# A two-layer decoder trunk: the indexer's queries of the first 128 tokens are no longer formed

## The chip, the cores and the metric

The kernel runs on one core of one Trainium2 chip. The metric is device time in microseconds (us) of one execution; a median of several executions is given. All times of single instructions come from one profiled execution.

## The reference, cut to what matters

The reference is two layers of a decoder for 512 tokens of width 1024, in float32. Each layer is a feed-forward block, a mixer with three attention branches that read one common input projection, and a second feed-forward block. The branch that matters here is A, a sparse attention: an indexer scores every key for every query, and each query attends only to its 128 best-scored keys.

```python
topk = min(INDEX_TOPK, S // 4)        # S = 512, so 128
...
qi = rope(qi.reshape(B, S, IDX_HEADS, IDX_DIM), cos, sin)     # 8 heads of 64
ki = rope(ki, cos, sin)
...
causal = s_pos[None, :] <= t[:, None]
logits = jnp.einsum('bqhd,bsd->bqhs', qib, ki)
iscore = jnp.einsum('bqhs,bqh->bqs', jax.nn.relu(logits).astype(jnp.float32), wib.astype(jnp.float32))
iscore = jnp.where(causal[None], iscore, -jnp.inf)
_, idx = lax.top_k(iscore, topk)
...
valid = (idx <= t[None, :, None])[:, None]
```

Query t has t + 1 causal keys. For the first 128 queries that is at most 128, so all of their causal keys are among the 128 picked ones, whatever the scores.

## The kernel before

**Tiles.** The 512 tokens are four tiles of 128 (`NT = 4`, tile number `t`). The width of 1024 is eight chunks of 128 (`KD = 8`, chunk number `k`). Activations and weights are kept as a high part and a low part (`hi`, `lo`, in the format F32R), and each float32 product is three matmuls: low times high, high times high, high times low.

**The mixer.** It first projects the normalised input, group of columns by group: `qi` (the indexer's queries, 512 columns), `ki` (the indexer's key, the values of branch B and the indexer's weights, 328 columns), `b`, `vc`, `c0` and so on. `project` loads the weights of a group in four pieces (`load_w`: one DMA on SyncE into `raw`, then ScalarE makes `hi` at L220 and VectorE makes `lo` at L221). There are four buffers each for `raw`, `hi` and `lo`, so the pieces of the next group can be split only once the last tile of the group before has read the old ones. Then, for each tile `t`, `project` issues 8 chunks of three matmuls (L755 to L757), 24 in all, into one of two PSUM banks.

**After a tile of `qi`.** ScalarE copies the bank out with the norm's factor (L919), GpSimd rotates it (`rope`, four instructions, L767 to L772), ScalarE and VectorE split it (L819, L820) and, some steps later, TensorE turns it with 8 transposes of 128x128 (L826, two PSUM banks of the tag `tr`). Eight casts then write the turned heads into the tiles of `qis`; `nc.any` at L829 divides them between ScalarE and VectorE. The counter `ready["i"]` goes up by one at each turned tile, of `qi` and of `ki`.

**The norm.** `n.advance` runs one stage after the first tile of `qi` (mean square, L309) and one after the second (broadcast, L327).

**Who reads `qis`.** Only `index_scores`, which starts when `ready["i"]` has its full count. Its loop already begins with tile 1: the mask of tile 0 is the causal mask, `masks = [causal_mask(0)]`.

**Order.** The order on each engine is the order in which the code issues instructions. A loop advances the projections by two chunks at a time and puts attention work and delayed steps (`defer`, counted in such steps) between them.

Of the kernel before, what the change touches and what calls it, by code (L numbers as in the profile page):

```python
# [23 lines left out]
NT = T // P  # L24
# [55 lines left out]
def trunk_kernel(ctx, tc, xt_in, pos_in, ng_in, wgu, wdn, wgrp, wgate, wbr_s, wbr_c, wo, qkg_in, lam_in, subg_in, out):  # L80
# [18 lines left out]
    def bank(tag="mm"):  # L99
        return ps.tile([P, 512], F32, tag=tag, name=nm(tag), bufs=BANKS[tag])  # L100

    def slot(dt=F32, tag="h", cols=512):
        return big.tile([P, cols], dt, tag=tag, name=nm(tag), bufs=SLOTS)

    def temp(tag, dt=F32, cols=512, bufs=2):
        return (phase[-1] if tag in ("p0", "p1", "pt", "e", "u") else tmp).tile([P, cols], dt, tag=tag, name=nm(tag), bufs=bufs)
# [105 lines left out]
    def load_w(src, cols, pieces=1):  # L212

        raw = wp.tile([P, WCOLS], F32, tag="raw", name=nm("raw"), bufs=RAW)
        hi = wp.tile([P, WCOLS], F32R, tag="hi", name=nm("hi"), bufs=HL)
        lo = wp.tile([P, WCOLS], F32R, tag="lo", name=nm("lo"), bufs=HL)
        for i in range(pieces):
            sl = slice(i * cols // pieces, (i + 1) * cols // pieces)
            nc.sync.dma_start(raw[:, sl], src[:, sl])
            S.activation(hi[:, sl], raw[:, sl], AF.Copy)  # L220
            V.tensor_tensor(lo[:, sl], raw[:, sl], hi[:, sl].bitcast(F32), op=ALU.subtract)  # L221
        return hi, lo
# [506 lines left out]
    def mixer(l, n, nxt, aside):  # L729
# [9 lines left out]
            tiles = [slot() for _ in range(NT // n_)]  # L739
            return lambda t: tiles[t // n_][:, (t % n_) * cols:(t % n_ + 1) * cols]  # L740

        def project(name):

            w_cols = len(GROUPS[name])
            kk_ = 2
            ws = []
            for k in range(0, KD, kk_):
                ws.append(load_w(wgrp[l, :, goff[name] + k * w_cols:goff[name] + (k + kk_) * w_cols], kk_ * w_cols))
            for t in range(NT):
                o = bank()  # L750
                for k in range(KD):
                    wh, wl = ws[k // kk_]
                    sl = slice((k % kk_) * w_cols, (k % kk_ + 1) * w_cols)
                    xh, xl = n.h[k][:, t * P:(t + 1) * P], n.l[k][:, t * P:(t + 1) * P]
                    PE.matmul(o[:, :w_cols], xl, wh[:, sl], start=k == 0, stop=False)  # L755
                    PE.matmul(o[:, :w_cols], xh, wh[:, sl], start=False, stop=False)  # L756
                    last_dense[0] = PE.matmul(o[:, :w_cols], xh, wl[:, sl], start=False, stop=k == KD - 1)  # L757
                    if k % 2 and k < KD - 1:
                        yield t, None
                yield t, o  # L760

        def rope(v, t, nh):

            a = sm.tile([P, 8, 16], F32, name=nm("ra"), tag="ra", bufs=2)
            b = sm.tile([P, 8, 16], F32, name=nm("rb_"), tag="rb_", bufs=2)
            ct = rc[:, t:t + 1, :].to_broadcast([P, nh, 16])
            G.tensor_tensor(a[:, :nh], v[:, :, :16], ct, op=ALU.mult)  # L767
            s0 = rs[:, t:t + 1, :8].to_broadcast([P, nh, 8])
            s1 = rs[:, t:t + 1, 8:].to_broadcast([P, nh, 8])
            G.tensor_tensor(b[:, :nh, :8], v[:, :, 8:16], s0, op=ALU.mult)  # L770
            G.tensor_tensor(b[:, :nh, 8:], v[:, :, :8], s1, op=ALU.mult)
            G.tensor_tensor(v[:, :, :16], a[:, :nh], b[:, :nh], op=ALU.add)  # L772
# [41 lines left out]
        def to_heads(v, nh, t, dst, lag, done):  # L814

            s = phase[-1].tile([P, 8, 2, HD], F32R, tag="st", name=nm("st"), bufs=ST)

            def split():
                S.activation(s[:, :nh, 0, :], v[:, :nh], AF.Copy)  # L819
                V.tensor_tensor(s[:, :nh, 1, :], v[:, :nh], s[:, :nh, 0, :].bitcast(F32), op=ALU.subtract)  # L820
                defer(LAG_H, turn)

            def turn():
                ps_ = [bank("tr") for _ in range(0, nh, 4)]
                for h in range(nh):
                    PE.transpose(ps_[h // 4][:, h % 4 * P:(h % 4 + 1) * P].bitcast(F32R),  # L826
                                 s[:, h].rearrange("p a d -> p (a d)"), ident_r)
                for h in sorted(range(nh), key=lambda h: (h % 4, h)):
                    nc.any.tensor_copy(dst[h][:, t * P:(t + 1) * P], ps_[h // 4][:, h % 4 * P:(h % 4 + 1) * P])  # L829
                done[0] += 1  # L830

            defer(lag, split)

        def swapped(src):
            d = slot(F32R)
            nc.sync.dma_start(d[:HD, :].bitcast(F32), src[HD:, :].bitcast(F32))
            nc.sync.dma_start(d[HD:, :].bitcast(F32), src[:HD, :].bitcast(F32))
            return d

        def scores(q, k1, k2, i):  # L840

            o = bank("sc")[:, :(i + 1) * P]
            ql = q[:, i * P:(i + 1) * P]
            PE.matmul(o, ql, k2[:, :(i + 1) * P], start=True, stop=False)  # L844
            PE.matmul(o, ql, k1[:, :(i + 1) * P], start=False, stop=True)
            return o
# [63 lines left out]
        va = phase[-1].tile([P, NT, HD], F32, tag="va", name=nm("va"), bufs=1)  # L910

        def dense_qi():
            for t, o in project("qi"):
                if o is None:
                    yield True
                    continue
                n.advance(last_dense[0])
                v = temp("t1", bufs=T1).rearrange("p (h d) -> p h d", d=HD)
                S.activation(v, o.rearrange("p (h d) -> p h d", d=HD), AF.Copy, scale=n.rn[:, t, :])  # L919
                rope(v, t, 8)  # L920
                to_heads(v, 8, t, qis, LAG_I, ready["i"])
                yield True

        def dense_ki():
            for t, o in project("ki"):
                if o is None:
                    yield True
                    continue
                v = temp("t1", bufs=T1).rearrange("p (h d) -> p h d", d=HD)
                S.activation(v[:, 0], o[:, :HD], AF.Copy, scale=n.rn[:, t, :])  # L930
                rope(v[:, :1], t, 1)
                to_heads(v, 1, t, kis, LAG_I, ready["i"])
                S.activation(vb(t), o[:, 64:320], AF.Copy, scale=n.rn[:, t, :])
                V.tensor_scalar(wi[:, t, :], o[:, 320:328], n.rn[:, t, :], 512 ** -0.5, op0=ALU.mult, op1=ALU.mult)
                yield True

        ready = {k: [0] for k in ("i", "b", "c0", "c1", "a")}

        def dense_qk(name, rows, qs, ks):
            for t, o in project(name):  # L940
                if o is None:
                    yield True
                    continue
                v = normed(o, t, [(base + rows[0], 4), (base + rows[1], 4)])
                to_heads(v, 8, t, qs + ks, LAG_N, ready[name])
                yield True
# [28 lines left out]
        def index_scores():  # L975
            ki2 = swapped(kis[0])
            for i in range(1, NT):
                w = (i + 1) * P
                acc = slot()
                for h in range(8):  # L980
                    o = scores(qis[h], kis[0], ki2, i)
                    r = temp("t2")
                    S.activation(r[:, :w], o, AF.Relu)
                    V.scalar_tensor_tensor(acc[:, :w], r[:, :w], wi[:, i, h:h + 1],
                                           causal[:, 512 - w:] if h == 0 else acc[:, :w], op0=ALU.mult, op1=ALU.add)
                    yield 1
                iscore.append(acc)
# [149 lines left out]
        def finished(b):  # L1137
# [10 lines left out]
        picks = choose()  # L1148
        ka2 = []
        work = deque([  # L1150
            (lambda: ready["i"][0] == 2 * NT, index_scores()),
            (lambda: ready["b"][0] == NT,
             attend("b", qb, kb, None, causal_mask, lambda j, h: vb(j)[:, h * HD:(h + 1) * HD], on_b)),
            (lambda: ready["c0"][0] == NT, attend_c(qc0, kc0, 0, on_c[:2])),
# [44 lines left out]
        for d in range(KD):  # L1199
# [3 lines left out]
            o = bank()  # L1203
# [16 lines left out]
    for l in range(DEPTH):  # L1220
        n1, n2 = Norm(3 * l + 1), Norm(3 * l + 2)
        n3 = Norm(3 * l + 3) if l + 1 < DEPTH else None
        aside = dram.tile([P, KD, T], F32, name=nm("aside"))
        with stage(f"ff{l}0"):
            ffn(l, 0, n, n1, aside, xt_in if l == 0 else None)
        with stage(f"mix{l}"):
            mixer(l, n1, n2, aside)
        with stage(f"ff{l}1"):
            ffn(l, 1, n2, n3)
        n = n3  # L1230
# [50 lines left out]
```

## Time and profile before

| | us |
|---|---|
| median of 3 executions | 2314.67 |
| lowest and highest of them | 2313.87 and 2317.65 |
| the profiled execution | 2315.78 |
| its span, first to last instruction | 2314.0 |
| TensorE (PE) busy in it | 2286.2 |
| VectorE (DVE) busy | 1721.5 |
| ScalarE (ACT) busy | 1117.9 |
| GpSimd (POOL) busy | 386.3 |

The span is what the trace shows; the execution's own time is a little longer. Busy time of TensorE is time in which at least one matmul is under way. The records of matmuls overlap: the next one starts before the record of the one before has ended, so the distance between starts, not the length of a record, is what a matmul takes of TensorE's time.

### The profile page before, as it was taken

The page shows a single profiled execution, that of the slowest core. Times are in us where ns is not written, and L with a number is a line of the kernel's source. Part 1 is how long each engine was busy: PE and PEld are TensorE (multiplying, and loading weights), DVE is VectorE, ACT ScalarE, POOL GpSimd, SP SyncE. Part 2 cuts the span into 40 slices and gives each one's busy share as a digit, 9 for nine tenths or more (in the row PEclk, how much of TensorE's full clock was granted, in tenths as well). Part 3 has the DMA queues.
Part 4 walks back from the last instruction along what each step waited for, and adds up shares of the span by engine and source line. Part 5 has one row for each costly group of instructions (what it writes and reads, how often), then busy time and mean ns, then how long its engine had stood idle before and what let it go on. Part 6 is the DMA issues. An engine that isn't in the chain of part 4 may idle for free.

```text
span 2314.0 us, 36117 instructions
## 1 busy us (share of the span) xinstructions
PE 2286.2 (99%) x13669; PEld 2013.8 (87%) x13669; DVE 1721.5 (74%) x3126; ACT 1117.9 (48%) x2129; POOL 386.3 (17%) x509
## 2 busy tenths in 40 slices
PE   9999999999999999999999999999999999999999
PEld 7899988887878889999889999888888887899997
DVE  7777765788875778777687777647889666777774
ACT  5444435666433444444444444446764344544442
POOL 0111101455010111101011101024641110110100
PEclk9999999999999999999999999999999999999999
DMA  4665524323232456555256555232322224655551
GB/s 161 176 162 157 143 68 137 101 76 101 74 96 73 141 146 164 159 147 153 66 156 167 157 146 156 84 125 74 101 74 82 88 91 137 159 153 147 157 137 64
DMA packets 111646, 286.74 MB, mean 124 GB/s; under 512 B 13168, under 2 KB 13168, under 8 KB 111472
## 3 DMA queue, kind: packets, MB, share of 16 engines
q1 hardware_dynamic: 90016, 246.00, 33.6%
q0 software_dynamic: 20736, 37.76, 9.7%
q8 instruction: 107, 1.75, 0.3%
q10 hardware_dynamic: 720, 0.68, 0.1%
q14 instruction: 67, 0.55, 0.1%
HBM read 270.76 MB, written 6.29 MB: 120 GB/s over the span
## 4 chain that ended last, share of the span: by engine, by line
PE 85%; DVE 7%; DMA 3%; ACT 2%; issue 1%; POOL 1%; SPq 0%; ACTq 0%; DVEq 0%; POOLq 0%
PE mm L227 11%; PE mm L229 10%; PE mm L228 10%; PE sc L227 8%; PE sc L229 8%; PE sc L228 8%; PE tr L227 5%; PE tr L229 5%; PE tr L228 5%; PE mm L755 4%; PE mm L756 3%; PE mm L757 3%; DMA h<-h 1%; PE sc L844 1%; DVE lo L344 1%
## 5 line engine op out<-in xcount | busy, mean ns | idle before, releaser
L227 PE MATMUL mm<-h,hi 128*128 128x512 f32 x1216 | 481.9, 396 | 1.4 <-DVE h L547 0.8
L229 PE MATMUL mm<-h,lo 128*128 128x512 f32 x1216 | 475.4, 391 | 4.3 <-DVE lo L344 4.3
L228 PE MATMUL mm<-h,hi 128*128 128x512 f32 x1216 | 474.5, 390 | 0.0
L452 POOL DMA_DIRECT2D sa<-in_wgu x144 | 126.8, 1051 | 931.4 <-DMA sa<-in_wgu 428.8
L229 PEld LDWEIGHTS mm<-h,lo 128*128 128x128 f32 x1216 | 228.3, 188 | 54.9 <-DVE lo L344 6.1
L344 DVE TENSOR_TENSOR lo<-raw,hi 128x1024 fp32r<-128x1024 f32 (+1 forms) x198 | 232.9, 1179 | 57.7 <-ACT hi L341 57.0
L227 PEld LDWEIGHTS mm<-h,hi 128*128 128x128 f32 x1216 | 228.4, 188 | 48.8 <-issue 4.8
L227 PE MATMUL sc<-h,hi 128*128 128x256 f32 (+1 forms) x832 | 265.4, 319 | 0.0
L229 PE MATMUL sc<-h,lo 128*128 128x256 f32 (+1 forms) x832 | 264.3, 318 | 0.0
L228 PEld LDWEIGHTS mm<-h,hi 128*128 128x128 f32 x1216 | 228.6, 188 | 41.0
L228 PE MATMUL sc<-h,hi 128*128 128x256 f32 (+1 forms) x832 | 264.1, 317 | 0.0
L341 ACT ACTIVATE hi<-raw 128x1024 fp32r<-128x1024 f32 (+1 forms) x198 | 200.7, 1020 | 92.0 <-PE tr L228 58.1
L227 PE MATMUL tr<-h,hi 128*128 128x256 f32 (+1 forms) x704 | 214.1, 304 | 5.0 <-DVE h L283 5.0
L229 PE MATMUL tr<-h,lo 128*128 128x256 f32 (+1 forms) x704 | 213.7, 303 | 0.0
L228 PE MATMUL tr<-h,hi 128*128 128x256 f32 (+1 forms) x704 | 213.5, 303 | 0.0
L220 ACT ACTIVATE hi<-raw 128x1024 fp32r<-128x1024 f32 (+2 forms) x136 | 139.6, 1029 | 99.2 <-PE mm L228 66.7
L221 DVE TENSOR_TENSOR lo<-raw,hi 128x1024 fp32r<-128x1024 f32 (+2 forms) x136 | 173.3, 1276 | 17.1 <-ACT hi L220 16.2
L755 PE MATMUL mm<-hi,h 128*128 128x512 f32 (+2 forms) x448 | 172.4, 385 | 0.0
L227 PEld LDWEIGHTS sc<-h,hi 128*128 128x128 f32 x832 | 159.3, 191 | 12.8 <-issue 0.3
L228 PEld LDWEIGHTS sc<-h,hi 128*128 128x128 f32 x832 | 159.2, 191 | 12.1
L229 PEld LDWEIGHTS sc<-h,lo 128*128 128x128 f32 x832 | 159.2, 191 | 11.1 <-DVE lo L570 0.4
L757 PE MATMUL mm<-lo,h 128*128 128x512 f32 (+2 forms) x448 | 167.0, 373 | 0.0
(337 smaller groups left out, 5063.8 us busy)
## 6 DMA issues: line engine op xcount, KB each, us to landing
raw<-in_wgu SPq DMA_DIRECT2D x102, 512.0 KB, 4.8
sa<-in_wgu SPq DMA_DIRECT2D x72, 512.0 KB, 3.9
sa<-in_wgu POOLq DMA_DIRECT2D x144, 256.0 KB, 5.8
raw<-in_wdn SPq DMA_DIRECT2D x128, 256.0 KB, 4.7
raw<-in_wgate SPq DMA_DIRECT2D x48, 512.0 KB, 3.5
raw<-in_wgrp SPq DMA_DIRECT2D x40, 512.0 KB, 4.5
a<-in_wgu SPq DMA_DIRECT2D x72, 256.0 KB, 5.1
raw<-in_wdn SPq DMA_DIRECT2D x32, 384.0 KB, 3.5
```

The source lines that it names most:

```text
L220: S.activation(hi[:, sl], raw[:, sl], AF.Copy)
L221: V.tensor_tensor(lo[:, sl], raw[:, sl], hi[:, sl].bitcast(F32), op=ALU.subtract)
L227: PE.matmul(o, ah, bl, start=first, stop=False, skip_group_check=onto)
L228: PE.matmul(o, ah, bh, start=False, stop=False, skip_group_check=onto)
L229: last_mm[0] = PE.matmul(o, al, bh, start=False, stop=last, skip_group_check=onto)
L341: S.activation(self.h, self.src, AF.Copy)
L344: V.tensor_tensor(self.l, self.src, self.h.bitcast(F32), op=ALU.subtract)
L452: G.dma_start(self.sa[:, j * 512:(j + 1) * 512], src[:, 1536:], accum_op=ALU.add)
L755: PE.matmul(o[:, :w_cols], xl, wh[:, sl], start=k == 0, stop=False)
L756: PE.matmul(o[:, :w_cols], xh, wh[:, sl], start=False, stop=False)
L757: last_dense[0] = PE.matmul(o[:, :w_cols], xh, wl[:, sl], start=False, stop=k == KD - 1)
L844: PE.matmul(o, ql, k2[:, :(i + 1) * P], start=True, stop=False)
```

## The change

The projection of `qi` runs over tiles 1 to 3 only, so for the tokens 0 to 127 the 24 matmuls, the copy out, the rotation, the split, the 8 transposes and the 8 casts are not issued, in each of the two layers. The weights of `qi` are loaded and split as before. The indexer's scores wait for seven turned tiles in place of eight. The output is the same function as before.

```diff
-        def project(name):
+        def project(name, tiles=range(NT)):
...
-            for t in range(NT):
+            for t in tiles:
                 o = bank()
...
         def dense_qi():
-            for t, o in project("qi"):
+            for t, o in project("qi", range(1, NT)):
...
-            (lambda: ready["i"][0] == 2 * NT, index_scores()),
+            (lambda: ready["i"][0] == 2 * NT - 1, index_scores()),
```

The order of the instructions shows what this makes of each engine. On TensorE, in the first layer, this is the end of the third projected tile of `qi` and what follows it, of before (`mm` is the PSUM bank of a projected tile, `hi` and `lo` the weights, `h` the activations, 128x512 the shape of the result):

```order
L757 MATMUL mm_3955<-lo_3860,h_3762 128x512
L755 MATMUL mm_4009<-hi_3841,h_3557 128x512
L756 MATMUL mm_4009<-hi_3841,h_3556 128x512
L757 MATMUL mm_4009<-lo_3842,h_3556 128x512
...
L826 MATMUL tr_4022<-ident_r,st_3954 128x128 x4
L826 MATMUL tr_4023<-ident_r,st_3954 128x128 x4
...
L757 MATMUL mm_4009<-lo_3860,h_3762 128x512
L755 MATMUL mm_4087<-hi_4064,h_3557 128x328
```

And the same place with the change:

```order
L757 MATMUL mm_3955<-lo_3860,h_3762 128x512
L755 MATMUL mm_4033<-hi_4010,h_3557 128x328
L756 MATMUL mm_4033<-hi_4010,h_3556 128x328
L757 MATMUL mm_4033<-lo_4011,h_3556 128x328
L755 MATMUL mm_4033<-hi_4010,h_3573 128x328
```

One block of 24 matmuls with 8 transposes in its middle is gone; the first matmul of `ki` (128x328) stands right behind the third projected tile, and apart from the numbers of the buffers every other row of TensorE stands as before, in both layers.

On ScalarE, from the copy of the second projected tile (L919) to the split of the second half of the `ki` weights, before (`tr` is a bank with turned heads, `raw` a loaded piece of weights, `st` the split tile ahead of its transposes):

```order
L919 ACTIVATE t_735_3946<-mm_3914,rn_3896 128x512
L329 ACTIVATE rb_3944<-tr_3941 128x512
...
L819 ACTIVATE st_3954<-t_735_3946 128x8x64
L919 ACTIVATE t_742_4000<-mm_3955,rn_3896 128x512
L220 ACTIVATE hi_4064<-raw_4063 128x656
L220 ACTIVATE hi_4070<-raw_4069 128x656
...
L819 ACTIVATE st_4008<-t_742_4000 128x8x64
L220 ACTIVATE hi_4076<-raw_4075 128x656
L220 ACTIVATE hi_4082<-raw_4081 128x656
L919 ACTIVATE t_749_4054<-mm_4009,rn_3896 128x512
```

With the change:

```order
L919 ACTIVATE t_735_3946<-mm_3914,rn_3896 128x512
L329 ACTIVATE rb_3944<-tr_3941 128x512
L220 ACTIVATE hi_4010<-raw_4009 128x656
L220 ACTIVATE hi_4016<-raw_4015 128x656
...
L819 ACTIVATE st_3954<-t_735_3946 128x8x64
L220 ACTIVATE hi_4022<-raw_4021 128x656
L220 ACTIVATE hi_4028<-raw_4027 128x656
L919 ACTIVATE t_742_4000<-mm_3955,rn_3896 128x512
```

The split of the `ki` weights now follows the copy of the second projected tile, not that of the third. Ahead of the last L819 row in each piece the casts (L829) of one turned tile are left out: five on ScalarE before, six with the change, since the eight casts of this tile are now divided six to two between ScalarE and VectorE, and before five to three. GpSimd loses the four rotations of one tile, and SyncE's order of DMAs is the same.

## Rows read from the trace of the kernel before

**Rows 1.** First lines of the page of before; last line: granted clock by slice.

```profile
span 2314.0 us, 36117 instructions
...
PE 2286.2 (99%) x13669; PEld 2013.8 (87%) x13669; DVE 1721.5 (74%) x3126; ACT 1117.9 (48%) x2129; POOL 386.3 (17%) x509
...
PEclk9999999999999999999999999999999999999999
```

**Rows 2.** Chain that ended last, shares of the span by engine.

```profile
PE 85%; DVE 7%; DMA 3%; ACT 2%; issue 1%; POOL 1%; SPq 0%; ACTq 0%; DVEq 0%; POOLq 0%
```

**Rows 3.** Waits of TensorE, whole run: us in total, times, longest.

```profile
PE tr L227 <- DVE h L283: 5.0, 4, 2.0
...
PE sc L844 <- DMA h<-h: 4.1, 8, 0.9
...
PE sc L227 <- ACT e L485: 1.9, 1, 1.9
```

**Rows 4.** TensorE's timeline, first layer: start us, length us of the record.

```profile
375.70 0.40 PE L755 MATMUL mm<-hi,h 128*128 128x512 f32 x1
...
378.45 0.79 PE L826 MATMUL tr<-ident_r,st 128*128 128x128 f32 x8
...
381.22 0.39 PE L755 MATMUL mm<-hi,h 128*128 128x512 f32 x1
381.44 0.39 PE L756 MATMUL mm<-hi,h 128*128 128x512 f32 x1
381.67 0.39 PE L757 MATMUL mm<-lo,h 128*128 128x512 f32 x1
381.90 0.39 PE L755 MATMUL mm<-hi,h 128*128 128x512 f32 x1
```

**Rows 5.** One-tile windows: length, busy PE, PEld, DVE, ACT, POOL; granted clock, DMA share, GB/s.

```profile
375.70:381.90 6.20, 6.20 (x34) 5.15 (x33) 1.57 (x4) 2.67 (x8) 1.49 (x4) 1.00 0.01 3
381.90:388.09 6.19, 6.19 (x34) 5.18 (x32) 3.92 (x7) 4.34 (x11) 1.48 (x4) 1.00 0.30 87
1522.01:1528.19 6.18, 6.18 (x34) 5.16 (x32) 1.56 (x4) 2.67 (x8) 1.49 (x4) 1.00 0.01 3
```

**Rows 6.** Groups by line and shape: busy us, mean ns of one.

```profile
L755 PE MATMUL mm<-hi,h 128*128 128x512 f32 x320 | 128.8, 402 | 0.0
...
L826 PE MATMUL tr<-ident_r,st 128*128 128x128 f32 x304 | 32.3, 243 | 0.0
```

**Rows 7.** SyncE's timeline and line L219 in 340:425, weight loads.

```profile
365.89 41.89 SPq L219 DMA_DIRECT2D raw<-in_wgrp  x9
...
DMA to landing us min/median/max: 3.0/4.8/6.9
```

**Rows 8.** Timelines of ScalarE, VectorE, TensorE around the change of groups.

```profile
385.45 0.94 ACT L829 CAST h<-tr 128x128 fp32r<-128x128 f32 x5
...
386.78 0.78 ACT L220 ACTIVATE hi<-raw 128x656 fp32r<-128x656 f32 x1
...
388.06 0.75 ACT L220 ACTIVATE hi<-raw 128x656 fp32r<-128x656 f32 x1 [0.51 <-PE mm L756]
...
387.59 0.84 DVE L221 TENSOR_TENSOR lo<-raw,hi 128x656 fp32r<-128x656 f32 x1
...
390.51 0.39 PE L755 MATMUL mm<-hi,h 128*128 128x328 f32 x1
```

**Rows 9.** Windows of 4 us in the first feed-forward, same columns as rows 5.

```profile
80.00:84.00 4.00, 3.08 (x20) 2.44 (x18) 2.72 (x5) 1.07 (x2) 0.00 (x0) 1.00 0.41 137
84.00:88.00 4.00, 3.06 (x16) 2.77 (x17) 3.28 (x5) 3.26 (x6) 0.00 (x0) 0.80 0.45 90
88.00:92.00 4.00, 4.00 (x16) 3.21 (x15) 2.40 (x4) 1.23 (x2) 1.66 (x2) 0.78 0.94 315
92.00:96.00 4.00, 4.00 (x19) 3.32 (x18) 3.96 (x6) 2.41 (x4) 0.07 (x1) 1.00 1.00 215
```

## The prediction

> **What bounds the kernel now.** I read the page first. TensorE is busy for 2286.2 of 2314.0 us, and the granted clock stands at its top digit in every slice [rows 1]. The chain that ended last, followed back from the final instruction, is TensorE for 85% of the span [rows 2]. So the kernel is one long in-order stream of matmuls, and what leaves this stream leaves the time, unless something else was about to be late at that place. TensorE idles for 27.8 us in all (2314.0 - 2286.2); its largest waits are 5.0 us for the norm's chunks (L283), 4.1 us in eight waits for the swapped keys that DMAs write (L844), and one of 1.9 us in the feed-forward [rows 3]. None of these stands at the projection of `qi`.
>
> Next I looked at the place itself. In the timeline the matmuls of a projected tile start at 381.22, 381.44, 381.67 and 381.90 us, each record 0.39 us long [rows 4]: the records overlap, and what a matmul costs the stream is the distance between starts, 0.68 / 3 = 0.227 us. In the windows one tile long TensorE is busy for the whole window, 6.20 of 6.20, at clock 1.00, while VectorE, ScalarE and GpSimd work for 1.57, 2.67 and 1.49 us of it [rows 5]. So TensorE is the engine that sets the pace here, and the other three have slack.
>
> **The change part by part.** *The block on TensorE.* The order of instructions shows that each layer loses one block of 24 matmuls of 128x512 with eight transposes in its middle, and that nothing else changes place on TensorE. Before, two such blocks of each layer have exactly this form, the third and the fourth tile of `qi`. The third starts at 375.70 and the next block at 381.90 [rows 4]: 6.20 us; the fourth takes 6.19, and the third of the second layer 6.18 [rows 5]. As a check from its parts: 24 x 0.227 = 5.45, and the transposes with the restart of the stream behind them take the other 0.75. I take 6.20 + 6.18 = 12.38 us for both layers. A lower bound is the matmuls alone, 2 x 5.45 = 10.9 us, as if the transposes had cost nothing.
>
> The Trainium skill states another price for such matmuls: "TensorE: Matmul & The Clock Gate", section "Back-to-back issue gap", gives some 131 ns for each matmul with 512 columns in a sustained stream, by which an estimate of the block is 24 x 0.131 + 0.75 = 3.9 us and of the two layers 7.8 us. The trace does not agree here: starts are 227 ns apart in it.
>
> *The work on the other engines.* One copy out, one split, one rotation of four instructions and eight casts go in each layer. They lie under TensorE's stream (1.57, 2.67 and 1.49 us of work in a tile of 6.20 [rows 5]), so I cost their removal at nothing; they would count only where TensorE waits for them, and in these windows it does not.
>
> *What comes earlier.* The weights of `ki` are now split one tile earlier, measured from the start of the mixer. Three things must keep up. First, their DMAs: the last of the four pieces is issued at 365.89, and the longest weight load of this stretch landed after 6.9 us [rows 7], so by 372.8. Its split on ScalarE began at 388.06 [rows 8], which becomes 388.06 - 6.2 = 381.9: 9 us of slack. Second, ScalarE: ahead of the third piece stand now six casts in place of five, and five took 0.94 us, from 385.45 on [rows 8], so the third split may come 0.3 us later than a plain shift. Its low part was ready at 387.59 + 0.84 = 388.43, and TensorE's first matmul that can read it began at 390.51 [rows 8]: 2.1 us of slack, 1.8 with the sixth cast. Third, the later loads: the nine that begin at 365.89 are spread over 41.89 us [rows 7], because each waits for a buffer that TensorE's stream sets free; they move with the stream. So I cost the earlier start at nothing. If the cover were gone, the split of a pair of pieces (0.78 and 0.84 us [rows 8]) would stand bare, 1.6 us for each layer, or 3.2 in all.
>
> *The sum.* The profiled execution took 2315.78 us, 1.78 more than its span, and 2315.78 - 12.38 = 2303.4. It is 1.11 above the median of the runs shown, 2314.67, so for the median I take 2314.67 - 12.38 = **2302.3 us**.
>
> **The rivals.**
>
> *A bare split at the change of groups.* The sixth cast, or a cast that waits for VectorE, delays the `hi` of the third piece until TensorE stands before the first tile of `ki`. For it: ScalarE and VectorE carry the casts of the first turned tile and the splits close together now. Against it: 1.8 us of slack. Price 3.2 us: 2305.5.
>
> *The gain is given back.* TensorE may wait later for something that does not move with it, above all the DMAs of the swapped keys (L844, up to 0.9 us each [rows 3]). For it: they are the one recurring wait behind `qi`. Against it: they start from casts of turned tiles, so from TensorE's own stream. To hide the gain it would have to give back 7.8 us, so that less than 4.6 (0.2% of 2314.67, about what a measurement of this kernel can tell from no change) is left: 2310 to 2315.
>
> *A block costs less than its window.* If the stream of matmuls were paced by the loading of weights alone, a block would be worth the 5.15 us that PEld is busy in it [rows 5], and 2 x 5.15 gives 2304.4. Against it: the block ends at the same distance from the next in three windows, and a removed block takes its whole distance with it.
>
> *Records taken as cost.* By the mean lengths of the records, 0.402 us for a matmul and 0.243 for a transpose [rows 6], a block would be worth 24 x 0.402 + 8 x 0.243 = 11.6 us, both 23.2, and the time 2291.5. The overlapping starts [rows 4] speak against it.
>
> *Slower: the weights of `ki` arrive late and TensorE cools.* The place is the first tile of `ki`. What a standstill does is seen early in the trace: in 80 to 88 us TensorE is busy only 3.08 and 3.06 of 4 us, and the granted clock falls to 0.80 and 0.78 in the 8 us from 84 on, before it is 1.00 again [rows 9]. These means lie between the two levels, 2.4 and 1.2 GHz; they cost 0.20 x 4 + 0.22 x 4 = 1.7 us, about as much as the standstill itself, 1.9 us [rows 3, 9]. So a bare wait costs up to double. To end above 2319.3 each layer would have to lose (12.4 + 4.6) / 2 = 8.5 us, that is a wait of some 4.3 us; with the slack of 9 us the last piece would have to land 13 us later than it does, some 20 us after its issue, against the 6.9 of the longest. That is the point from which it decides, and nothing in the trace comes near it.
>
> On the cooling the Trainium skill says the same: "TensorE: Matmul & The Clock Gate", section "HAM oscillation — how this bites in real kernels", has the array fall back to its slow level when it idles for a DMA, and the matmuls behind the wait pay for it. The trace agrees with its 0.80 and 0.78.
>
> **How the numbers follow.** Forecast 0.88 (2302.3; 2300 to 2305 with the scatter of runs); bare split 0.04 (2305.5); given back 0.03; cheaper block 0.02 (2304.4); records 0.01; slower 0.02. That the change does not do what it says is not among them: the order shows the block gone. Faster by over 0.2%: 0.88 + 0.04 + 0.02 + 0.01 = 0.95, of which I move 0.01 to no change for what I have not seen: 0.94; within 0.2%: 0.04; slower: 0.02. The range reaches down to the lowest run shown less the sum and half of the waits for swapped keys, 2313.87 - 12.38 - 2.0 = 2299.5, since waits in the rest of the stream may also fall away by chance, and up to the bare split with half a microsecond of scatter, 2306.0.
>
> **What would show it.** Right: the span is shorter by 11 to 13 us and busy TensorE by about as much; 48 matmuls and 16 transposes fewer; idle TensorE stays at 27 to 29 us; the third projected tile of `qi` is followed by the first 128x328 matmul without a wait; and the time from the start of the mixer to that matmul is 6.2 us shorter in each layer. Wrong: a wait of TensorE for `lo` or `hi` of L220 and L221 at the first tile of `ki`, or for the casts' banks at L826; a clock below 1.00 there; or longer waits at L844 than the 4.1 us of before. The prediction fails if idle TensorE grows by more than some 4 us, or if the block gone is not worth its window.

## The result, and the profile after

The changed kernel takes 2301.04 us in the median of six executions (2295.15 to 2301.65). The kernel before, run beside it, took 2312.98 (2311.2 to 2317.65, with the three shown earlier). The ratio is 0.9944, with a 95% interval of 0.9933 to 0.9955: 10.4 to 15.5 us faster. The forecast of 2302.3 us lies 1.3 above the measured median. Two executions of a later version (the tables' loads moved to SyncE), one of them the profiled one of its first run, were heavily disturbed, and no number here is from them.

The first rows of the page after, in answer to [rows 1], and its chain that ended last, in answer to [rows 2]:

```profile
span 2299.7 us, 35955 instructions
...
PE 2272.8 (99%) x13605; PEld 2002.7 (87%) x13605; DVE 1717.4 (75%) x3116; ACT 1113.3 (48%) x2117; POOL 382.5 (17%) x501
...
PEclk9999999999999999999999999999999999999999
...
PE 89%; DVE 6%; DMA 2%; ACT 1%; issue 1%; POOL 1%; SPq 0%; DVEq 0%; ACTq 0%; POOLq 0%
```

The span is 14.3 us shorter and TensorE's busy time 13.4 us; idle TensorE is 26.9 us (2299.7 - 2272.8), where it was 27.8.

TensorE's timeline of the last projected tile of `qi` in the first layer, in answer to [rows 4] (start, length of the record):

```profile
374.10 0.40 PE L755 MATMUL mm<-hi,h 128*128 128x512 f32 x1
...
376.85 0.79 PE L826 MATMUL tr<-ident_r,st 128*128 128x128 f32 x8
...
379.61 0.39 PE L755 MATMUL mm<-hi,h 128*128 128x512 f32 x1
379.84 0.39 PE L756 MATMUL mm<-hi,h 128*128 128x512 f32 x1
380.07 0.39 PE L757 MATMUL mm<-lo,h 128*128 128x512 f32 x1
380.29 0.31 PE L755 MATMUL mm<-hi,h 128*128 128x328 f32 x1
```

The starts are still 0.23 us apart, and the first matmul of `ki` (128x328) follows the last one of `qi` at that same distance, without a wait. The windows of this tile and of its counterpart in the second layer, in answer to [rows 5] (length, busy time of PE, PEld, DVE, ACT and POOL, granted clock, DMA share, GB/s):

```profile
374.10:380.29 6.19, 6.19 (x33) 5.16 (x32) 3.04 (x6) 4.81 (x13) 1.48 (x4) 1.00 0.33 93
1515.44:1521.62 6.18, 6.18 (x34) 5.16 (x32) 3.03 (x6) 4.83 (x13) 1.48 (x4) 1.00 0.30 89
```

A tile still takes 6.2 us. ScalarE now works 4.81 us in it, which is more than the 4.34 it had at the change of groups [rows 5], with two instructions more, the sixth cast one of them; TensorE is busy for all of it. The groups by line and shape, in answer to [rows 6]:

```profile
L755 PE MATMUL mm<-hi,h 128*128 128x512 f32 x304 | 123.0, 405 | 0.0
...
L826 PE MATMUL tr<-ident_r,st 128*128 128x128 f32 x288 | 30.7, 243 | 0.0
```

Sixteen matmuls of line L755 fewer, and with L756 and L757 that makes 48, and sixteen transposes fewer. The timelines of ScalarE, VectorE and TensorE around the change of groups, in answer to [rows 8]:

```profile
377.68 1.24 ACT L829 CAST h<-tr 128x128 fp32r<-128x128 f32 x6
...
379.35 0.74 ACT L220 ACTIVATE hi<-raw 128x656 fp32r<-128x656 f32 x1
...
380.12 1.77 DVE L221 TENSOR_TENSOR lo<-raw,hi 128x656 fp32r<-128x656 f32 x2
...
382.72 0.39 PE L755 MATMUL mm<-hi,h 128*128 128x328 f32 x1
```

The third piece of the `ki` weights has its `hi` at 380.09 and its `lo` at about 381.0 (half of the two splits that begin at 380.12); TensorE reads it from 382.72 on: 1.7 us of slack, where the forecast had 1.8.

**Where the 14.3 us are.** I split both spans at the start of the mixer and at the first matmul of `ki`; I call the stretch between them the run-in.

| stretch | before | after | difference |
|---|---|---|---|
| start to the first mixer | 363.39 | 361.70 | -1.69 |
| run-in, layer 0 | 24.70 | 18.59 | -6.11 |
| to the second mixer | 1121.61 | 1122.84 | +1.23 |
| run-in, layer 1 | 24.65 | 18.49 | -6.16 |
| to the end | 779.65 | 778.08 | -1.57 |

The two run-ins give 12.27 us, the sum that was forecast as 12.38. The other 2.0 us lie where both kernels run the same instructions in the same order, and the granted clock explains most of them. Windows of before in which the clock was below 1.00:

```profile
10.00:20.00 10.00, 9.84 (x36) 7.99 (x37) 8.59 (x14) 9.21 (x15) 0.00 (x0) 0.83 0.85 325
80.00:90.00 10.00, 8.14 (x41) 6.78 (x40) 8.00 (x12) 4.33 (x7) 0.00 (x0) 0.83 0.52 153
1960.00:1970.00 10.00, 8.76 (x38) 6.88 (x37) 6.61 (x13) 5.32 (x10) 1.35 (x2) 0.86 0.29 96
1970.00:1980.00 10.00, 10.00 (x44) 8.20 (x43) 7.97 (x15) 3.86 (x6) 3.24 (x4) 0.97 0.93 211
```

And of the changed kernel:

```profile
10.00:20.00 10.00, 9.61 (x36) 7.84 (x37) 8.78 (x14) 9.34 (x16) 0.00 (x0) 0.83 0.87 320
510.00:520.00 10.00, 8.10 (x42) 6.42 (x39) 7.29 (x24) 4.74 (x16) 6.68 (x12) 0.83 0.99 287
```

What such a window loses is (1 - clock) x its length: 1.7 + 1.7 + 1.4 + 0.3 = 5.1 us before, 1.7 + 1.7 = 3.4 us after. I call 1.7 us a dip. At the full clock throughout, the spans would be 2308.9 and 2296.3 us, 12.6 apart, of which the run-ins are 12.27. The waits of TensorE after the change, in answer to [rows 3]:

```profile
PE tr L227 <- DVE h L283: 4.3, 4, 1.6
PE sc L844 <- DMA h<-h: 3.5, 4, 1.9
...
PE sc L227 <- ACT e L485: 1.6, 1, 1.6
```

TensorE waits for swapped keys in four places where it was eight, and for 3.5 us in all where it was 4.1. But the longest of these waits grew from 0.9 to 1.9 us. It stands in the first layer, 134 us behind the last tile of `qi`, and the dip of 510 to 520 us lies on it. In TensorE's timeline, and on the line that issues the swaps (L836):

```profile
514.68 0.30 PE L844 MATMUL sc<-h,h 128*128 128x128 f32 x1 [1.90 <-DMA h<-h]
```

```profile
DMA to landing us min/median/max: 6.1/6.2/6.2
```

The same place in the kernel before:

```profile
521.68 0.30 PE L844 MATMUL sc<-h,h 128*128 128x128 f32 x1 [0.72 <-DMA h<-h]
```

```profile
DMA to landing us min/median/max: 4.6/4.8/5.0
```

It waited 0.72 us, its swaps landed after 4.6 to 5.0 us, and its clock stayed at 1.00. So about 1.2 us of wait and 1.7 us of dip are new here, 2.9 us that the projection had gained. The stretch between the run-ins grew by 1.23 all the same, not by 2.9, because other waits in it became shorter: those for swapped keys come to 2.4 us in this stretch in both traces. Runs 8 and 9 below take this up.

### The profile page after: what moved, and what is told of

The parts are those of the page before. It is cut to its first block, busy times and chain, and to the rows that moved or that the text cites. A ratio compares the mean times of both kernels' runs of the same rounds, so it can differ in the third digit from the quotient of the medians.

```text
span 2299.7 us, 35955 instructions
## 1 busy us (share of the span) xinstructions
PE 2272.8 (99%) x13605; PEld 2002.7 (87%) x13605; DVE 1717.4 (75%) x3116; ACT 1113.3 (48%) x2117; POOL 382.5 (17%) x501
## 4 chain that ended last, share of the span: by engine, by line
PE 89%; DVE 6%; DMA 2%; ACT 1%; issue 1%; POOL 1%; SPq 0%; DVEq 0%; ACTq 0%; POOLq 0%
PE mm L227 11%; PE mm L229 11%; PE mm L228 11%; PE sc L227 8%; PE sc L229 8%; PE sc L228 8%; PE tr L227 5%; PE tr L228 5%; PE tr L229 5%; PE mm L755 4%; PE mm L757 4%; PE mm L756 4%; PE sc L844 1%; PE sc L845 1%; PE tr L867 1%
## 5 line engine op out<-in xcount | busy, mean ns | idle before, releaser
L220 ACT ACTIVATE hi<-raw 128x1024 fp32r<-128x1024 f32 (+2 forms) x136 | 139.5, 1028 | 97.2 <-PE mm L228 65.6
L221 DVE TENSOR_TENSOR lo<-raw,hi 128x1024 fp32r<-128x1024 f32 (+2 forms) x136 | 172.7, 1271 | 17.8 <-ACT hi L220 17.0
L229 PEld LDWEIGHTS sc<-h,lo 128*128 128x128 f32 x832 | 158.6, 191 | 10.9 <-DVE lo L570 0.4
L755 PE MATMUL mm<-hi,h 128*128 128x512 f32 (+2 forms) x432 | 166.7, 386 | 0.0
L227 PE MATMUL sc<-h,qhi 128*128 128x256 f32 x576 | 162.7, 282 | 3.6 <-DVE u L495 2.0
```

The costliest lines, as they stand in the source:

```text
L227: PE.matmul(o, ah, bl, start=first, stop=False, skip_group_check=onto)
L229: last_mm[0] = PE.matmul(o, al, bh, start=False, stop=last, skip_group_check=onto)
```

## The experiments

The spans below are also given less their dips, which I summed over windows of 10 us of each trace as above; it is the better measure of an edit of a few us, since the executions of the kernel before lie 4 to 9 us apart in each set measured here.

**1. The matmuls kept.** In the loop of `dense_qi`:

```diff
-            for t, o in project("qi", range(1, NT)):
+            for t, o in project("qi"):
                 if o is None:
                     yield True
                     continue
+                if t == 0:
+                    yield True
+                    continue
```

> The changed kernel with the 24 matmuls of tile 0 put back in each layer; their result is not read, and the copy, rotation, split, transposes and casts of tile 0 stay left out. Run-in means the time from the first matmul of the qi projection to the first of ki (24.70 and 24.65 us before, 18.59 and 18.49 with the change). Forecast's theory (a matmul costs the distance between starts, 0.227 us): run-in 18.5 + 24 x 0.227 = 24.0 us, so about 1.4 us below the kernel before in all and 10.9 above the changed one. Rival, records taken as cost (0.402 us each): run-in 28.2. Rival, cheaper block (paced by weight loads of 0.188 us): run-in 23.0. If it were the work on the other engines that had cost the time, the run-in would stay near 18.5.

Measured: 2313.34 us, ratio to before 1.0002 (0.9992 to 1.0012); the run-ins are 23.95 and 23.93 us. TensorE's timeline, the first matmul of the mixer and the last of `qi` with the first of `ki`:

```profile
360.15 0.39 PE L755 MATMUL mm<-hi,h 128*128 128x512 f32 x1
...
383.87 0.39 PE L757 MATMUL mm<-lo,h 128*128 128x512 f32 x1
384.10 0.31 PE L755 MATMUL mm<-hi,h 128*128 128x328 f32 x1
```

The 24 matmuls cost 23.95 - 18.59 = 5.36 and 23.93 - 18.49 = 5.44 us, the 24 x 0.227 of the forecast. Records as cost (28.2) and the weight loads as pace (23.0) are both off, and so is the thought that the other engines' work had cost the time: all of it was left out here, and 10.8 of 12.3 us of the run-ins came back. In the whole time the interval holds the -1.4 us that this leaves (0.9994).

**2. The turn kept.** Behind tile 1's `to_heads`, with `ready["i"]` counted to eight again:

```diff
                 to_heads(v, 8, t, qis, LAG_I, ready["i"])
+                if t == 1:
+                    to_heads(v, 8, 0, qis, LAG_I + 2, ready["i"])
```

> The complement of the run with the matmuls kept: no matmuls for tile 0, but eight transposes and eight casts more, made from the copy of tile 1 and written where tile 0's heads would stand (nothing reads them), so tile 0's rotation is left out and its split done on other data. Forecast's theory: the transposes with the restart of the stream cost 0.75 us, run-in 19.3, all in all 1.5 us above the changed kernel. Rival, bare work on ScalarE and VectorE (one more split and eight more casts in the shorter run-in): a wait of TensorE for the split tile or for the splits of the ki weights, run-in 20 us or more. Rival, records (8 x 0.243): 20.4 without a wait in the trace.

Measured: ratio 0.9949 (0.9933 to 0.9965), run-ins 19.16 and 19.12 us. The turn costs 0.57 and 0.63 us, somewhat under the 0.75 that the window left for it, and no wait at L820, L221 or L826 stands in the trace. With the first run the two halves of the block are 5.4 + 0.6 = 6.0 us, of the 6.1 to 6.2 that both cost together.

**3. Half the width.** `project` takes 256 of the 512 columns for tile 0, and four heads are turned:

```diff
+                cols = 256 if name == "qi" and t == 0 else w_cols
...
-                    sl = slice((k % kk_) * w_cols, (k % kk_ + 1) * w_cols)
+                    sl = slice((k % kk_) * w_cols, (k % kk_) * w_cols + cols)
...
-                    PE.matmul(o[:, :w_cols], xl, wh[:, sl], start=k == 0, stop=False)
+                    PE.matmul(o[:, :cols], xl, wh[:, sl], start=k == 0, stop=False)
```

> Tile 0 of qi is projected again, but only 256 of its 512 columns (four of the eight heads, four transposes); the other four heads of tile 0 are left out. Nothing reads either. Forecast's theory, with 0.12 us between starts as the 128x256 matmuls of the index scores show: run-in 18.5 + 24 x 0.12 + 0.4 = 21.8 us, some 6.6 us above the changed kernel in all. Rival, cheaper block (a matmul costs its weight load of 0.188 us, whatever its columns): run-in 18.5 + 24 x 0.188 + 0.4 = 23.4 us, some 9.8 us above the changed kernel.

Measured: 2311.49 us, ratio to before 0.9996 (0.9985 to 1.0008). The run-in of layer 0 is 22.07 us, near the 21.8 of columns as cost. That of layer 1 is 24.73, and the whole time shows no gain that can be told from none: the two run-ins together are 2.55 us shorter than before, which lies inside the interval. TensorE's waits, and its timeline in layer 1, show what happened there (L756 to L758 are L755 to L757 of the other kernels, one line lower):

```profile
PE mm L758 <- DVE lo L221: 0.9, 1, 0.9
```

```profile
1512.91 0.28 PE L756 MATMUL mm<-hi,h 128*128 128x256 f32 x1
...
1514.26 0.39 PE L758 MATMUL mm<-lo,h 128*128 128x256 f32 x1 [0.95 <-DVE lo L221]
...
1517.22 0.63 PE L758 MATMUL mm<-lo,h 128*128 128x512 f32 x1
1517.65 0.63 PE L756 MATMUL mm<-hi,h 128*128 128x512 f32 x1
```

The faster tile reaches the last piece of the `qi` weights before its `lo` is ready: a wait of 0.95 us. From 1517 on the records are 0.63 us long and 0.43 us apart, nearly twice the usual distance, which is the lower level of the clock. The window shows it (columns as above):

```profile
1510.00:1520.00 10.00, 9.05 (x49) 7.61 (x48) 7.30 (x12) 3.86 (x6) 2.49 (x4) 0.84 0.46 145
```

The dip of 1.6 us and the wait of 0.95 make the 2.66 us by which this run-in exceeds the other. So a wait does end on the path here, and it is dearer than itself. The profiled execution carries 11.9 us of dips in all, so most of them lie elsewhere.

**4. Half the width, second.** The same with tile 0 behind tile 1:

```diff
-            for t, o in project("qi"):
+            for t, o in project("qi", (1, 0, 2, 3)):
```

> The half-width tile 0 again (256 of its 512 columns, four heads, read by nothing), but projected second, behind tile 1. Theory: the run with the half-width tile first gained nothing over the kernel before because its 0.12 us matmuls reach the last piece of the qi weights before it is split (a wait of 0.95 us for lo at L221 in the second layer), and TensorE's clock fell behind that wait; placed second, the weights are there, the run-in is 18.5 + 24 x 0.12 + 0.4 = 21.8 us in both layers, no wait at L221, and the time lies some 6.6 us above the changed kernel and 5.8 below the kernel before (ratio about 0.9975). Rival, a matmul costs its weight load of 0.188 us: run-in 23.4, ratio about 0.9988. Rival, narrow matmuls cool the clock by themselves: granted clock below 1.00 in the windows of the run-in, without a wait.

Measured: run-ins 22.02 us in both layers, no wait at L221, clock 1.00 throughout the first of them:

```profile
361.00:384.00 23.00, 22.97 (x125) 19.49 (x124) 11.85 (x21) 10.75 (x23) 5.71 (x13) 1.00 0.26 80
1960.00:1970.00 10.00, 10.00 (x34) 8.26 (x35) 9.13 (x18) 4.81 (x8) 4.59 (x5) 0.67 0.51 117
```

That settles the price for this block: columns count, the weight load does not set the pace, and the narrow matmuls alone did not lower the granted clock. The whole time did not follow: 2310.55 us, ratio 0.999 (0.9981 to 1.0), where 0.9975 was expected. The profiled execution carries 8.5 us of dips, so 2309.5 - 8.5 = 2301.0 is 4.7 above the changed kernel's 2296.3. They stand at 0 to 20, 810 to 820 and 1950 to 1970 us (the second row above), far from the edit. Those at 810 and 1960 us follow waits of 1.42 and 2.06 us for the norm's chunks (L283), which come to 6.0 us here and to 4.3 in the changed kernel:

```profile
PE tr L227 <- DVE h L283: 6.0, 4, 2.1
```

The mean granted clock of its eleven executions was 0.996 to 1.000, that of the seventeen of before beside it 0.997 to 1.000 with most at 0.999. Why this kernel waits longer there and takes more dips, I could not settle.

**5. Two tiles out.** `project("qi", range(2, NT))`, and in `index_scores`:

```diff
-                    o = scores(qis[h], kis[0], ki2, i)
+                    o = scores(qis[h], kis[0], ki2, i, max(i, 2))
```

> Tile 1 of qi is left out as well as tile 0, and the scores of tokens 128 to 255 are formed with the queries of tile 2, so the picks of those tokens are not the reference's; the number of matmuls there is unchanged. Forecast's theory: the splits of the ki weights have 9 us of slack for their DMAs before the change, 2.9 after two steps of 6.2, so they are hidden still: run-in 12.4 us, 12.4 us below the changed kernel, ratio to before about 0.989. Rival, bare split: a wait of TensorE before the first ki tile, run-in 14 us or more, gain of the second step 9 us or less.

Measured (with `ready["i"]` counted to six): 2287.32 us, ratio 0.9885 (0.9866 to 0.9905), run-ins 12.31 us in both layers. The second tile is worth what the first was, and no wait took its place.

**6. Three tiles out.** The same with 3 in place of 2, and the norm's second stage run behind the first tile of `ki`:

```diff
             for t, o in project("ki"):
...
+                if t == 0:
+                    n.advance(last_dense[0])
```

> Only tile 3 of qi is projected; scores of tokens 128 to 383 are formed with the queries of tile 3, so their picks are not the reference's, with the number of matmuls there unchanged. The norm's broadcast moves behind the first ki tile. Forecast's theory of the cover: the slack of 9 us for the last piece of the ki weights is used up after 12.4 us of earlier start, so here a wait must show: the last piece lands 7 to 9.4 us after the start of the mixer and its split would be due at 6.1, so TensorE waits 1 to 5 us at the first ki tile for lo or hi, run-in or first ki tile longer by that, and the clock may fall behind it. Rival, the cover is nowhere near used up (weights land much earlier or are not needed then): run-in 6.2 us, no wait, 24.7 us below the changed kernel.

Measured: 2272.83 us, ratio 0.9834 (0.9821 to 0.9847), run-ins 6.25 us, no dip in the trace, and no wait at L220 or L221. My expectation failed and its rival held. The timelines of VectorE and TensorE show the last piece of the `ki` weights:

```profile
367.40 0.84 DVE L221 TENSOR_TENSOR lo<-raw,hi 128x656 fp32r<-128x656 f32 x1
...
368.61 0.31 PE L755 MATMUL mm<-hi,h 128*128 128x328 f32 x1
...
368.91 0.31 PE L757 MATMUL mm<-lo,h 128*128 128x328 f32 x1
```

The last split ends at 368.24. The seventh chunk, the first to read this piece, starts at 368.61 and reads `lo` at 368.91, so 0.7 us of cover is left. I had counted when the split could begin and forgot that TensorE needs it only six chunks, 18 matmuls of 0.15 us or 2.8 us, into the tile.

**7. The tables' loads on SyncE.** Four small loads in the first feed-forward sit in ScalarE's queue while TensorE waits for L485:

```diff
-        nc.scalar.dma_start(posi, pos_in)
-        nc.scalar.dma_start(subg, subg_in)
+        nc.sync.dma_start(posi, pos_in)
+        nc.sync.dma_start(subg, subg_in)
```

(and the two above them in the same way). On the changed kernel:

> The changed kernel with the four small loads of the tables (L150 to L155) issued by SyncE in place of ScalarE; nothing is left out. Theory: their issue holds ScalarE's queue for 3 us (80.43 to 83.4 us in the trace of before), TensorE waits 1.9 us behind it (L485) and in the trace of before its clock falls to 0.80 and 0.78 for 8 us, in that of the changed kernel not; without them the wait goes: 1.6 to 3.6 us below the changed kernel, and the mixer starts at 358 to 360 us. Rival: the wait stands anyway, since the weights or VectorE are late there: no change. Rival on the other side: four more DMAs on SyncE's queue delay the weight loads behind them, and a later wait of 1 us or more takes its place.

Measured: ratio to before 0.9941 (0.9928 to 0.9955). On the kernel before:

> The kernel before with that one edit alone (the tables' loads on SyncE); nothing is left out. Theory: 1.9 to 3.6 us below the kernel before, the wait at L485 gone from the list of waits, the clock at 1.00 from 20 us to the mixer. Rival: no change, or a new wait for weights.

Measured: ratio 0.9993 (0.9984 to 1.0002); the wait at L485 falls from 1.9 to 0.2 us and the clock is 1.00 from 20 us to the mixer, which starts at 360.08. The span less its dips is 2308.3 - 1.7 = 2306.6, against 2308.9. Both once more, side by side:

> The changed kernel, unaltered, on the same chip as the version with the tables' loads on SyncE, so that the two can be compared. Theory: executions differ by how many dips of the clock they carry (1.7 us each; two in the profiled execution of the changed kernel, three in that of before), so the span less what the dips cost is 2296.3 us in this profile as in the last, within 2 us, and the times lie on 2296 to 2302. Rival: the scatter has another source, and the span less the dips differs by 3 us or more. The run-in is 18.5 us in both layers.

> The changed kernel with the tables' four loads issued by SyncE, once more, since its profile fell on a disturbed execution. Theory: the wait at L485 (1.6 to 1.9 us) is gone, and with it one of the places where the clock dips; 1.6 us below the changed kernel in the span less the dips (2294.7), 2 to 3 us in the median of the runs. Rival: no difference, as for the kernel before with the same edit (ratio 0.9993, interval 0.9984 to 1.0002).

Measured: the changed kernel 0.9945 (0.9932 to 0.9958), with one dip, and 2297.1 - 1.7 = 2295.4 us less dips, where its first profile gave 2296.3: the dips explain 1.7 of the 2.6 us between its two spans. With the loads moved 0.9939 (0.9925 to 0.9954), and 2299.8 - 5.1 = 2294.7. In that trace the wait at L485 is gone and the stretch behind it runs at full clock, but there are three dips' worth elsewhere (two in the first 20 us, one at 510 to 520) and 5.6 us of waits for swapped keys, where there were 3.5:

```profile
80.00:90.00 10.00, 10.00 (x58) 8.78 (x57) 9.88 (x15) 6.18 (x11) 0.00 (x0) 1.00 0.36 120
```

```profile
PE sc L844 <- DMA h<-h: 5.6, 6, 2.4
```

That the edit took the wait away is not shown. Run 1 has no wait at L485 and run 8 one of 0.3 us, with the four loads still on ScalarE. ScalarE's queue shows the difference; the second of the four loads in the trace of before, and in that of run 1:

```profile
80.80 1.62 ACTq L152 DMA_DIRECT2D lp<-in_lam  x1
```

```profile
80.30 0.45 ACTq L152 DMA_DIRECT2D lp<-in_lam  x1
```

In nine of the eleven traces with the loads on ScalarE one of the four, not always the same, takes 1.14 to 1.80 us to issue, and the wait is 0.7 to 2.2 us; in runs 1 and 8 none takes over 0.45. So the wait goes with one slow issue, and not with the four loads standing there. Why one issue is slow stays open, and whether the edit shortens the time, these intervals cannot tell.

**8 and 9. The swapped keys in the first layer** (8 with 32 matmuls, 9 with 6). The wait of 1.90 us shown above came again in the second profile of the changed kernel (1.83 us) and in that with the loads moved (2.38), each time with a dip. In all three a packet of the queue that fetches instructions lay on the DMA engines among the swaps. The queues of the changed kernel in the microsecond from 511 on (packets, MB, share of 16 engines):

```profile
q1 hardware_dynamic: 124, 0.21, 99.6%
q8 instruction: 1, 0.02, 8.2%
```

In run 2, where no wait stands there, that packet came before the swaps. Two runs move the changed kernel's stream against those packets, by 32 or 6 one-column matmuls at its very start, behind the warm-up matmuls (all lines are two lower):

```diff
+    for _ in range(32):
+        PE.matmul(idle[:, :1], zeros[:, :P], zeros[:, :1], start=True, stop=True)
```

> The changed kernel with 32 narrow matmuls (one column, result unread) more at the very start, where TensorE waits for data anyway; they make up for the 32 matmul and weight-load pairs that the change takes out of TensorE's program ahead of the attention of layer 0. Theory: in all three profiles of the changed kernel and in none of the others, a packet of TensorE's instructions (queue q8) falls among the DMAs of the swapped keys some 130 us behind the qi projection; those DMAs then land after 6.2 us in place of 5, TensorE waits 1.8 to 2.4 us for them in place of 0.7 or less, and the clock dips. With the 32 pairs back the packet comes some 5 us earlier, as before: wait at that place 0.7 us or less, no dip behind it, clock 1.00 at 510 to 530 us, and up to 2.9 us below the changed kernel (ratio to before about 0.9932). Rival: the wait has another cause and stays at 1.8 us or more (ratio about 0.9944). Rival: the packet hits other DMAs elsewhere, and the time stays where it was though this wait is gone.

> The same with only 6 narrow matmuls at the start, as a control. Theory: six pairs move the packet by about 1 us, so it still falls among the DMAs of the swapped keys; the wait stays at 1.5 us or more, with the dip behind it, and the time stays that of the changed kernel (ratio about 0.9944). Rival: narrow matmuls at the start help by themselves (the clock, or the timing of the start); then this run shows a short wait or a shorter time as well.

Measured: 2299.39 us, ratio to before 0.9946 (0.9934 to 0.9958), with 32; 2297.05 us, 0.9938 (0.9926 to 0.9949), with 6. With 32 the wait in the first layer is gone and the clock there is 1.00, but a wait of 2.10 us for swapped keys with a dip stands in the second layer, where there was none. Windows, and TensorE's timeline:

```profile
505.00:525.00 20.00, 19.50 (x119) 16.31 (x118) 17.66 (x52) 13.08 (x39) 13.44 (x20) 1.00 0.54 159
1650.00:1660.00 10.00, 8.38 (x37) 7.12 (x38) 6.76 (x29) 5.42 (x19) 3.55 (x8) 0.83 0.61 191
```

```profile
1651.62 0.33 PE L846 MATMUL sc<-h,h 128*128 128x128 f32 x1 [2.10 <-DMA h<-h]
```

A fetched packet lies among the swaps there too. They are issued from 1644.51 us on and land after 6.3 to 6.5 us (L838), and this is the queue between 1648 and 1649 us:

```profile
q8 instruction: 1, 0.02, 7.0%
```

So the last rival in the expectation of run 8 held: the packet met other swaps, with a wait and a dip, and the time stayed where it was. In the first layer, where no packet fell among them, the swaps landed after 4.1 to 4.5 us.

With 6 the fetched packet moved to between 504 and 505 us, ahead of the swaps, which begin at 506.81: it moved by more than I had meant, so this run is no control with the packet left in place. The wait stays, at 1.58 us, without a dip. The queue between 504 and 505 us, and TensorE's timeline:

```profile
q8 instruction: 1, 0.02, 8.3%
```

```profile
513.38 0.30 PE L846 MATMUL sc<-h,h 128*128 128x128 f32 x1 [1.58 <-DMA h<-h]
```

Its swaps landed after 5.0 to 5.9 us. So each of the four waits of 1.8 us or more for swapped keys comes with a fetched packet among the swaps and with landings of 5.9 to 6.8 us, and no other trace has a packet among the swaps of this place in either layer. But the wait of 1.58 us comes without one, and in run 6 a packet lies among later swaps, at 553 us, without a wait. The packet can be a cause of the late landings, and it is not the only one; no run changes it alone, so this is argued and not shown. What the first of the two shows is that this loss moves about with the stream: a shift at the start of the program took it from one layer and put it into the other, and the time did not follow.

## Why the prediction was right, point by point

- **TensorE's stream sets the time, and a block costs its window.** Shown. The run-ins fell by 6.11 and 6.16 us against 6.20 and 6.18, and putting back the matmuls or the turn alone gives back 5.4 and 0.6 us each layer. The lower bound of 10.9 us for the matmuls alone was measured as 10.8.
- **The other engines' work is hidden.** Shown by run 1, in which it is left out and only 1.4 to 1.5 us of the gain remain. Run 2 puts 1.2 of these at the transposes with their split and casts; the remaining 0.3 us is not assigned.
- **The earlier start of the `ki` weights costs nothing.** Right. The slack behind the sixth cast came out at 1.7 us (forecast 1.8), and the cover lasted for two more tiles (runs 5 and 6). The 9 us of slack for the last piece was counted to the start of its split and not to the matmul that reads it; so I expected a wait in run 6, wrongly.
- **The bare split.** It did not come. Run 3 shows what it would have been like, at a neighbouring place: 0.95 us of wait.
- **The gain given back.** A part of it was, and at the line that I named: 2.9 us at one wait for swapped keys in the first layer. The sum of those waits fell all the same (3.5 us for 4.1), and the dips of before at 80 to 90 and at 1960 to 1980 us are not in this trace, so the whole time does not show it. That these cancel is luck; the prediction has no term for either. The rival would have needed 7.8 us. My sign against it, that the swaps start from TensorE's own stream and move with it, held for their issue; it did not hold for their landing, which took 6.1 to 6.2 us where it had been 4.6 to 5.0.
- **The cheaper block and the records as cost.** Both fell, with runs 1, 3 and 4: matmuls cost 0.227 us at 512 columns and 0.12 at 256. The figure of 131 ns in the Trainium skill ("TensorE: Matmul & The Clock Gate", section "Back-to-back issue gap") does not hold for the 512 columns of this kernel in any of these traces.
- **Slower, by a wait that cools TensorE.** It did not come, and its price was mis-sized in the prediction. I put a bare wait at up to double itself. The runs show a loss in steps of 1.7 us that does not grow evenly with the wait: 1.6 us behind 0.95 (run 3), 1.7 behind 1.90, 2.10 and 2.38 (the waits for swapped keys), and two steps, 3.4, behind 2.06 (run 4). A short wait can so cost nearly three times itself; if no more than one or two steps follow a longer wait, which no run here shows, the wait from which that rival decides is by an estimate 8.5 less 1.7 or 3.4, or 5.1 to 6.8 us, not 4.3.
- **The number.** 2302.3 against 2301.04. The forecast took the median of three executions of before (2314.67); with six it is 2312.98. The two medians lie 11.94 us apart and the ratio gives 12.95; the forecast of 12.38 lies between them. The run-ins, 12.27 us, are the firmer proof.
- **Signs that did not come as stated.** The span was to be 11 to 13 us shorter and idle TensorE to stay at 27 to 29 us; they came out at 14.3 and 26.9. The dips account for 1.7 us of the span, which leaves 12.6; the prediction did not count them in this sign.

## What to carry to other kernels

Where one engine is busy all the time and in order, price a removal by the distance between the starts of its instructions in the very window that goes, not by the length of their records. Then ask what is fetched during the removed work, and count its slack to the instruction that reads it, not to the one that prepares it. A faster tile is not always a gain: in the second layer the half-width tile ran into its weights, paid for the wait once more, and dearer, through the clock, and ended where the full one did.

## What was not expected of the hardware

The granted clock falls in steps that lose about 1.7 us each, and one kernel's executions carry different numbers of them: 5.1 and 3.4 us in the first two profiles, none in run 6, 11.9 in run 3, 8.5 in run 4. Apart from those in the first 20 us, each of them in the thirteen traces used here lies on or just behind a standstill of TensorE: the waits at L485 and for swapped keys, that at L221 in run 3, and those for the norm's chunks at 810 to 830 and at 1940 to 1970 us. All twelve standstills of 1.8 us or more have one, and so have those of 0.95 (run 3), 1.24 (before, 1965 us) and 1.42 us (run 4). The other standstills under 1.8 us have none, that of 1.58 us in run 9 and one of 1.66 at L485 in run 6 among them. At L485 TensorE waited 1.9 us in the trace of before and its clock fell, and 1.6 us in that after, where the windows of 84 to 92 us stay at 1.00, against 0.80 and 0.78 in [rows 9]:

```profile
84.00:88.00 4.00, 3.26 (x20) 2.97 (x21) 3.49 (x5) 3.06 (x6) 0.00 (x0) 1.00 0.31 62
88.00:92.00 4.00, 4.00 (x20) 3.30 (x19) 3.95 (x6) 2.10 (x3) 1.67 (x2) 1.00 0.96 340
```

At L485 the waits of 1.86, 1.91 (run 3) and 2.19 us (run 2) come with a dip and the shorter ones without; at the other places 0.95 us was enough. What decides among the shorter waits, I could not settle.
